# A hybrid RWKV-7 and DeltaNet block: a planner's landing times for loads, the order of its queue, and a read-back in pieces

## The chip, the cores and the metric

The kernel runs on one core of one Trainium2 chip. The metric is the time of one execution on the device in microseconds (us), the median of several. Engines are called PE (matrix products), DVE (vector), ACT (scalar, activations), POOL and SP; SP does nothing here but issue transfers.

## The reference

One layer of a diffusion backbone over 256 latent and 256 context tokens of width 2048, all in float32.

```python
mod = silu(c) @ w_ada + b_ada            # shifts, scales and gates of both halves
h  = modulate(rmsnorm(x, norm1_w), sh1, sc1)
hc = modulate(rmsnorm(ctx, norm1_w), csh1, csc1)
rw, cv, z, ab, gt = split(h @ w_in)      # and the same of hc
# branch 1: RWKV-7, 16 heads of 64, two directions, context scan first
s = s * w_t - (s @ kk_t) b_t^T + v_t k_t^T ;  y_t = s @ r_t
# branch 2: gated DeltaNet, 8 heads of 128, chunks of 64, two directions
sol = triangular_solve(I + lmat, [v*beta, k*beta*exp(g)])
v_new = u_i - w_i @ s ;  o = qd_i @ s + qk_i @ v_new ;  s = s * gl + kt_i^T @ v_new
m = sigmoid(g_a) * (o_a @ p_a) + sigmoid(g_b) * (o_b @ p_b)
x = x + gt1 * (m @ w_out)
x = x + gt2 * (silu(gate) * up) @ w_down # SwiGLU, hidden 5632
return rmsnorm(x, final_norm_w)
```

## The kernel before, in words

Every float32 product with a weight is done as three products of rounded halves: `whi` is the weight rounded by ACT, `wlo` the rest, subtracted by DVE, and the activation is split in the same way; PE multiplies whi with both halves and wlo with the first.

The program has four parts. First come the modulation of the first norm and the low-rank products (to about 125 us of the profile). Then a planned stretch (lines 1150 to 1830, 125 to 1340 us) does the input projection, both branches with their scans, and the first products of the merge. Then comes the rest of the merge with the output projection (to 1500 us), and last the feed-forward network (to the end). The last two are in a fixed order.

The planned stretch is written as some hundred generators, called pieces, each with a rank. The class `Weave` (line 218) runs them while the program is built: each yields its next operation, the planner keeps a clock for each engine and each piece, and at every step it takes the operation that could start first, the smaller rank first among equals. So a table of costs, `LAT` in line 31, sets the order in which PE, DVE, ACT and POOL run their instructions. On the chip each engine keeps to its row and waits by semaphores. A piece that yields a number waits for so long in planned time. The order of SP's queue is not the planner's own: it is made by the library's scheduler, which follows the order in which the issues are written and what they need.

`Loads` (line 168) stands for the queue. Called, it issues the transfer at once, and returns the planned time to its landing: from the later of now and the queue's free time, the bytes at 360 KB a us, and `LAT["dma"]`.

Pieces that the change touches:

- `fetch` and `cast` (lines 1156, 1164): weights come in quarters of 128x512 (256 KB) into a ring of buffers `raws`; ACT then makes whi (`his`) and DVE wlo (`los`).
- `gate_out` (1148): a product of the gates' columns is copied by ACT and stored to `gts_` in DRAM; `merge_gates` reads the gates back as `gts`.
- `merge_in` (1194): reads branch 1's output `oad` from DRAM into `PA` and splits it with `both` (a copy on ACT, a subtraction on DVE), so that the products with `pa` can start. Those with `pb`, branch 2, follow when its last head is done.
- `ada_early` (1754) and `ada_rest` with `row_tile` (1771): the rest of the modulation. Each transfer brings a row block of `ada_rest`, which DVE multiplies by an entry of `ck` and adds to the last one; there are 96 of 128x512 (tile `wraw`) and then 48 of 128x1024 (tile `aw`), all of rank 500. The early ones use two spare tiles, which afterwards go into the ring `raws` (it has three until then, and a third spare joins later).
- `invert` (635): the triangular inversions, with round trips through DRAM (`scr`, `tscr`).
- `head_inverse`, `head_scan`: a DeltaNet head's inversion, and its scan in four steps, in which PE (`s<-gvt,TF`, `s<-St,arena`), DVE (`Vn`), PE (`s<-Vn,kta`) and DVE (`St`) take turns, and `s<-Qe,St` with `s<-aw,Vn` give the output; `s<-arena,CR` then sums squares for the norm.

In names `out<-in,in` the products with a weight are `mm<-x,whi` and `mm<-x,wlo`; `ob` is branch 2's output. Line 164 is that of a helper which records every operation of a piece, line 175 that of `Loads`.

Of the kernel before, what the change touches and what calls it, by code (L numbers as in the profile page):

```python
# [27 lines left out]
NHELD, NB = 6, 10  # L28
GATES_A, GATES_B = ((36,0,0,0,0,0,0,0),(0,0,0,0,0,4,0,0))

LAT = dict(dma=3.1, v=1.0, s=1.0, hop=dict(e=0.215, v=0.135, s=0.15, g=0.1), slack=0.1, own=0.09, grp=32, crank=-1, cg=4, into=0.14, back=0.2, cross=0.14, stay=0.0, gpace=1.6)
LNEXP = "natural_log_exp_and_others"
SIGM = "sigmoid_and_others"
UNIT = 64 * 64 + 64
# [53 lines left out]
class Places:  # L88


    def __init__(self, pool, arena, *tags):
        self.pool, self.slots, at = pool, {}, 0
        for tag, n, bufs in tags:
            self.slots[tag] = itertools.cycle([arena[:, at + n * i:at + n * i + n] for i in range(bufs)])
            at += n * bufs
# [17 lines left out]
class Lane:  # L113


    def __init__(self, engine, fixed, each, own, hop):
        self.engine, self.fixed, self.each, self.own, self.hop, self.base = engine, fixed, each, own, hop + LAT["slack"], None

# [49 lines left out]
class Loads:  # L168
# [5 lines left out]
    def __call__(self, out, src, slow=1.0):  # L174
        self.queue.dma_start(out, src)
        cost = int(np.prod(out.shape)) * 4 / 360e3 * slow
        self.free = max(self.free, weave.now) + cost
        return self.free + LAT["dma"] - weave.now

# [38 lines left out]
class Weave:  # L218
# [52 lines left out]
    def turn(self, mode):  # L271
        return 0.0 if mode == self.mode else LAT["back"] if mode == "full" else LAT["into"] if self.mode == "full" else LAT["cross"]

    def run(self):
        while self.work:
# [4 lines left out]
            for w in self.work:  # L280
# [4 lines left out]
                elif isinstance(w.want, list):  # L285
                    lane = w.want[0].lane
                    start = max(self.free.get(lane, 0.0), w.at(lane))
                    if lane is self.tensor and self.mode != "full" and w.want[0].mode == "full":
                        start += LAT["stay"]
                    key = (start, w.rank)  # L290
# [16 lines left out]
            if lane is self.tensor:  # L307
                ops, rest = ops[:LAT['grp']], ops[LAT['grp']:]
                if self.mode == "full" and ops[0].mode == "full" and start > self.free.get(lane, 0.0) + 0.02:
# [19 lines left out]
def emit(ctx: ExitStack, tc, A, out, dbg=None):  # L329
    nc = tc.nc  # L330
    V, S, G, Q = nc.vector, nc.scalar, nc.gpsimd, nc.sync
    E = nc.tensor
    global weave
    weave = Weave()
    dq = Loads(Q)
    e, v, s, g = (Lane(x, fixed, each, LAT["own"], LAT["hop"][n]) for x, fixed, each, n in
                  ((E, 0.0, 0.0, "e"), (V, 0.07, 0.00104, "v"), (S, 0.06, 0.0009, "s"), (G, 0.06, 0.0022, "g")))
    e.own = 0.0
# [136 lines left out]
    with tc.tile_pool(name="p0", bufs=1) as p0, \  # L475
# [78 lines left out]
        def low_split(e):  # L554
            res = []
            for k in range(2):
                pool = p0 if e % 2 else wp
                pair = []
                for t in ("whi", "wlo"):
                    if t == "wlo" and e == k == 0:  # L560
                        V.memset(wp.tile([P, 32], F32, tag="wpad", name="wpad", bufs=1), 0.0)
                    pair.append(pool.tile([P, 8, P] if pool is wp else [P, NL], F32R, tag=f"{t}{k}" if pool is p0 else t, name=t,
                                          bufs=1 if pool is p0 else 2))
                hi, lo = pair
                if pool is wp:
                    hi, lo = (t.rearrange("p k m -> p (k m)")[:, :NL] for t in (hi, lo))
                S.copy(hi, lws[e][k])
                V.tensor_sub(lo, lws[e][k], hi.bitcast(F32))
                res.append((hi, lo))
            return res  # L570
# [13 lines left out]
        for part in range(NE + 1):  # L584
            if part < NE:
                ps = pst(pmm, "mm")
            for c in range(4):
# [4 lines left out]
                if c == 0 and part < NE:  # L592
                    w = low_split(part)
# [152 lines left out]
    oad = dpool.tile([8, P, T], F32, name="oad")  # L746
# [401 lines left out]
    def gate_out(pool, j, ps):  # L1148
        g = pool.tile([P, T], F32, tag="gt", name="gt")
        yield s.copy(g, ps[:, :T])  # L1150
        weave.release(mmb)
        Q.dma_start(gts_[j], g)
        if j == 39:
            weave.ready("gates")

    def fetch(parts, i):

        for q, part in enumerate(parts):
            raw = yield raws
            landed[i, q] = raw, weave.now + dq(raw[:, :part.shape[1]], part)  # L1160
            weave.ready("asked", i, q)
            yield 0.0
# [24 lines left out]
    OA, OB, PA, gts = [], [], [], []  # L1187

    def both(dst, src, i, n):

        yield s.copy(dst[0][:, i:i + n], src)
        yield v.tensor_sub(dst[1][:, i:i + n], src, dst[0][:, i:i + n].bitcast(F32))

    def merge_in():

        yield "out", NPAIR - 1
        for what in "KV":
            yield what + "gemm", NGH - 1
        oa = hx.tile([P, 2, 8, T], F32R, tag="ch", name="oa")
        OA.extend((oa[:, 0], oa[:, 1]))  # L1200
        PA.append(hx.tile([P, KT, T], F32, tag="cl", name="PA"))
        yield dq(PA[0][:, 0:8], oad.rearrange("k p t -> p k t"))
        for i in range(0, 8, 2):
            yield from both(OA, PA[0][:, i:i + 2], i, 2)
        weave.ready("merge")

# [48 lines left out]
    def products():  # L1255
# [53 lines left out]
        while todo or ahead:  # L1309
# [62 lines left out]
            if what == "g":  # L1372
                weave.add(150, gate_out(rs, p, ps))
            elif what == "p":
                weave.add(150, first_merge(p, ps, p == KT - 1))
            else:
                (hd if what in "KVQ" else pr)[p][what + "ps"] = ps
                weave.ready(what + "gemm", p)
# [360 lines left out]
    def ada_sum(b, nj, acc, arow):  # L1739

        m = 2 * nj
        ps = yield pab
        yield [e.matmul(ps[32 * j:32 * j + 32, 0:T], ones[:, 0:32], acc[:, T * j:T * j + T], start=True, stop=True)
               for j in range(nj)]
        weave.ready("block", b)
        r = slice(0, 32 * nj)
        yield v.tensor_copy(arow[r], ps[r, 0:T])
        yield [e.transpose(ps[:, T + P * q:T + P * q + 32 * nj], arow[r, P * q:P * q + P], ident[r, r]) for q in range(2)]
        for q in range(2):
            o = slice(32 + b + q, 32 + b + m, 2)  # L1750
            yield v.tensor_add(mod[:, o], ps[:, T + P * q:T + P * q + 32 * nj:32], p_("bada")[:, o])
        weave.release(pab)

    def ada_early():

        yield ("spare",)
        ws = [t.rearrange("p k m -> p (k m)") for t in spare[:2]]
        for b in range(NEARLY):
            for k in range(KT):
                w, last = ws[k % 2], ws[1 - k % 2]  # L1760
                yield dq(w, A["ada_rest"][b // 2, :, k, 512 * (b % 2):512 * (b % 2) + 512])
                if k:
                    yield v.scalar_tensor_tensor(w, w, ck[:, k, 0:1], last, ALU.mult, ALU.add)
                else:
                    yield s.activation(w, w, AF.Identity, scale=ck[:, 0, 0:1])
            yield from ada_sum(4 * b, 2, w, last[:, 0:T])
        raws.put(*spare[:2])
        yield "turned", NPAIR - 1
        raws.put(spare[2])

    def ada_rest():
        yield ("places",)
        yield "out", NPAIR - 1
        acc, kx = [gs.tile([P, 1024], F32, tag="KBc", name="aw") for _ in range(2)]
        ws = [gs.tile([P, 1024], F32, tag="KBm", name="aw") for _ in range(2)]
        for i in (0, 512):
            PTs.append(kx[:, i:i + 512].rearrange("p (d b c) -> p d b c", d=2, b=2))
        weave.ready("extra")
        arow = gs.tile([P, T], F32, tag="arow", name="arow")
        early = NEARLY // 2  # L1780

        def row_tile(i):
            b, k = divmod(i, KT)
            w = ws[i % len(ws)]
            yield dq(w, A["ada_rest"][b, :, k, :])
            if k == 0 and b > early:
                yield "block", 8 * (b - 1)
            if k:
                yield "added", i - 1
            for n in (0, 512):  # L1790
                a = acc[:, n:n + 512]
                if k:
                    yield v.scalar_tensor_tensor(a, w[:, n:n + 512], ck[:, k, 0:1], a, ALU.mult, ALU.add)
                else:
                    yield s.activation(a, w[:, n:n + 512], AF.Identity, scale=ck[:, 0, 0:1])
            weave.ready("added", i)

        for i in range(early * KT, 6 * KT):
            if i > early * KT + 1:
                yield "added", i - 2  # L1800
            weave.add(500, row_tile(i))
            if i % KT == KT - 1:
                yield "added", i
                weave.add(500, ada_sum(8 * (i // KT), 4, acc, arow))
# [28 lines left out]
    PA = PA[0]  # L1833
# [35 lines left out]
    with tc.manual_schedule(engines={mybir.EngineType.PE, mybir.EngineType.DVE, mybir.EngineType.Activation,  # L1869
# [18 lines left out]
        for j in range(KT):  # L1888
# [7 lines left out]
            k, a = divmod(j, 4)  # L1896
            raw = zap.tile([P, CG, P], F32, tag="wr", name="wr", bufs=2)
            k = slice(CG * k, CG * k + CG)
# [10 lines left out]
    with tc.tile_pool(name="fp", bufs=1, reuse_waits="tile") as fp:  # L1909
# [19 lines left out]
        for j in range(NH):  # L1929
# [6 lines left out]
            g = fp.tile([P, T], F32, tag="g", name="g", bufs=2)  # L1936
# [5 lines left out]
            if 2 <= j < 34:  # L1942

                for a in range(2):
                    c = (j - 2) // 2
                    i = 2 * (j % 2) + a
                    w = fp.tile([P, 512], F32, tag="aw", name="aw", bufs=3)
# [119 lines left out]
```

## Time and profile before

| what | value |
|---|---|
| median of 3 runs (lowest to highest) | 2208.12 us (2203.57 to 2210.75) |
| the profiled execution | 2211.11 us |
| its span | 2209.3 us |
| mean granted clock of PE | 0.986 |
| busy share of PE, DVE, ACT, POOL | 96%, 70%, 51%, 1% |

The span is the time between the first and the last instruction that the profile shows; busy shares are of the span. The granted clock is a share of the full one. A wait is shown at the instruction that waited, behind an arrow the engine and the tile that came last. `SPq` is SP's queue, PEld the loading of weights into PE.

### The profile page before, as it was taken

Reading aid. Unit: us, or ns where it says so; the run is one execution under the profiler, and the core shown is the slowest. Engines: PE = TensorE matmul, PEld = TensorE weight load, DVE = VectorE, ACT = ScalarE, POOL = GpSimd, SP = SyncE. Lnnn points to the kernel's source line nnn. Section 1 sums busy time; section 2 is a strip of 40 time slices with the busy share of each in tenths; the row PEclk is TensorE's granted clock in tenths of the full one; section 3 lists DMA queues with packets and bytes.
Section 4 is the critical chain, followed back from the end, with each engine's and each line's share of the span. In section 5 each row is a group of like instructions: output and inputs, shape, how many; then the busy total and the mean of one; then the engine's idle time right before and its main releaser. Section 6 shows DMA issues by size and latency. Waiting matters only on the chain. (4 is left out here: it accounts for less than half of the span.)

```text
span 2209.3 us, 59354 instructions
## 1 busy us (share of the span) xinstructions
PE 2124.0 (96%) x24654; PEld 1993.5 (90%) x24654; DVE 1554.4 (70%) x3318; ACT 1128.3 (51%) x2220; POOL 19.3 (1%) x55
## 2 busy tenths in 40 slices
PE   7999999999999999999999898999999999999998
PEld 4997698888899888898899898999999999999997
DVE  3466588888889877788888876765666665545554
ACT  3246554565556456655556564654444444444443
POOL 0000000000000000000000000000000000000000
PEclk9999999999999999999999999999999999999999
DMA  9966756645555564655556934846777776666665
GB/s 382 411 165 197 220 155 177 182 140 158 153 162 155 162 182 126 170 176 148 152 156 181 301 109 148 255 156 190 234 239 239 238 238 216 194 192 192 194 197 164
DMA packets 276286, 431.15 MB, mean 195 GB/s; under 512 B 119856, under 2 KB 136624, under 8 KB 271664
## 3 DMA queue, kind: packets, MB, share of 16 engines
q1 hardware_dynamic: 262192, 402.19, 59.3%
q10 hardware_dynamic: 13824, 25.17, 3.6%
q8 instruction: 193, 3.16, 0.6%
q14 instruction: 77, 0.63, 0.1%
HBM read 401.50 MB, written 25.77 MB: 193 GB/s over the span
## 5 line engine op out<-in xcount | busy, mean ns | idle before, releaser
L427 DVE TENSOR_TENSOR wlo<-wraw,whi 128x1024 fp32r<-128x1024 f32 (+1 forms) x264 | 315.0, 1193 | 297.3 <-ACT whi L426 297.1
L426 ACT CAST whi<-wraw 128x1024 fp32r<-128x1024 f32 (+1 forms) x264 | 270.6, 1025 | 391.0 <-PE mm L437 344.6
L164 PE MATMUL mm<-hxh,wlo 128*128 128x256 f32 x1376 | 401.8, 292 | 6.3 <-DVE wlo L164 5.8
L164 PE MATMUL mm<-hxh,whi 128*128 128x256 f32 x1376 | 398.2, 289 | 3.6 <-ACT whi L164 2.7
L164 PE MATMUL mm<-hxl,whi 128*128 128x256 f32 x1376 | 395.9, 288 | 0.2 <-issue 0.2
L438 PE MATMUL mm<-hfh,wlo 128*128 128x256 f32 x1344 | 372.8, 277 | 2.9 <-DVE wlo L427 2.9
L436 PE MATMUL mm<-hfh,whi 128*128 128x256 f32 x1344 | 371.2, 276 | 0.0
L437 PE MATMUL mm<-hfl,whi 128*128 128x256 f32 x1344 | 371.2, 276 | 0.0
L164 ACT CAST whi<-wraw 128x512 fp32r<-128x512 f32 (+1 forms) x398 | 243.1, 615 | 195.5 <-PE mm L164 80.0
L164 DVE TENSOR_TENSOR wlo<-wraw,whi 128x512 fp32r<-128x512 f32 (+1 forms) x398 | 269.7, 681 | 90.5 <-ACT whi L164 87.7
L164 PEld LDWEIGHTS mm<-hxh,wlo 128*128 128x128 f32 x1376 | 261.9, 190 | 18.4 <-DVE wlo L164 9.4
L164 PEld LDWEIGHTS mm<-hxh,whi 128*128 128x128 f32 x1376 | 261.7, 190 | 12.5 <-issue 4.5
L164 PEld LDWEIGHTS mm<-hxl,whi 128*128 128x128 f32 x1376 | 261.7, 190 | 5.9 <-issue 3.4
L438 PEld LDWEIGHTS mm<-hfh,wlo 128*128 128x128 f32 x1344 | 252.4, 188 | 5.1 <-DVE wlo L427 4.9
L437 PEld LDWEIGHTS mm<-hfl,whi 128*128 128x128 f32 x1344 | 252.5, 188 | 0.0
L436 PEld LDWEIGHTS mm<-hfh,whi 128*128 128x128 f32 x1344 | 252.5, 188 | 0.0
L164 PE MATMUL mm<-hch,wlo 128*128 128x256 f32 x496 | 143.5, 289 | 0.0
L164 PE MATMUL mm<-hch,whi 128*128 128x256 f32 x496 | 142.8, 288 | 0.0
L164 PE MATMUL mm<-hcl,whi 128*128 128x256 f32 x496 | 141.9, 286 | 0.1
L436 PE MATMUL mm<-za,whi 128*128 128x256 f32 x512 | 141.5, 276 | 0.0
L438 PE MATMUL mm<-za,wlo 128*128 128x256 f32 x512 | 141.3, 276 | 0.0
L437 PE MATMUL mm<-za,whi 128*128 128x256 f32 x512 | 141.3, 276 | 0.0
(399 smaller groups left out, 4585.9 us busy)
## 6 DMA issues: line engine op xcount, KB each, us to landing
wraw<-w SPq DMA_DIRECT2D x344, 256.0 KB, 3.3
wraw<-wgu SPq DMA_DIRECT2D x168, 512.0 KB, 4.8
aw<-ada_first SPq DMA_DIRECT2D x32, 1024.0 KB, 10.9
wraw<-wdn SPq DMA_DIRECT2D x64, 448.0 KB, 3.6
wraw<-ada_rest SPq DMA_DIRECT2D x96, 256.0 KB, 3.2
aw<-ada_rest SPq DMA_DIRECT2D x48, 512.0 KB, 4.2
wraw<-wout SPq DMA_DIRECT2D x64, 256.0 KB, 4.2
aw<-ada_gt ACTq DMA_DIRECT2D x64, 256.0 KB, 5.1
```

Source lines behind the costliest of these rows:

```text
L164: return Op(self, cost, lambda: getattr(self.engine, name)(out, *a, **k), mode, base)
L426: S.copy(hi[:, c, :M], raw[:, c, :M])
L427: V.tensor_sub(lo[:, c, :M], raw[:, c, :M], hi[:, c, :M].bitcast(F32))
L436: E.matmul(ps, hi, Xh[:, k, :n], start=first and i == 0, stop=False)
L437: E.matmul(ps, hi, Xl[:, k, :n], start=False, stop=False)
L438: E.matmul(ps, lo, Xh[:, k, :n], start=False, stop=last and i == len(wt) - 1)
```

## The change

All loads are counted as landing 0.5 us later (`dma` 3.1 to 3.6), and rows of the modulation 1.5 us later still (`late`). A `yield 0.0` ahead of an issue gives the turn back to the planner, so that the issues are written in the order of planned time; this is done for the weights, the gates' stores and the modulation rows. `gq` is the same queue as `dq`. The read-back of branch 1 is four transfers of two slices, each followed by its split, where it was one of eight slices.

```diff
-LAT = dict(dma=3.1, ..., gpace=1.6)
+LAT = dict(dma=3.6, ..., gpace=1.6, late=1.5)
...
-    dq = Loads(Q)
+    dq = gq = Loads(Q)
...
         yield s.copy(g, ps[:, :T])
         weave.release(mmb)
+        yield 0.0
         Q.dma_start(gts_[j], g)
...
             raw = yield raws
+            yield 0.0
             landed[i, q] = raw, weave.now + dq(raw[:, :part.shape[1]], part)
...
-        yield dq(PA[0][:, 0:8], oad.rearrange("k p t -> p k t"))
         for i in range(0, 8, 2):
+            yield dq(PA[0][:, i:i + 2], oad[i:i + 2].rearrange("k p t -> p k t"))
             yield from both(OA, PA[0][:, i:i + 2], i, 2)
...
                 w, last = ws[k % 2], ws[1 - k % 2]
-                yield dq(w, A["ada_rest"][b // 2, :, k, 512 * (b % 2):512 * (b % 2) + 512])
+                yield 0.0
+                yield LAT["late"] + gq(w, A["ada_rest"][b // 2, :, k, 512 * (b % 2):512 * (b % 2) + 512])
...
             w = ws[i % len(ws)]
-            yield dq(w, A["ada_rest"][b, :, k, :])
+            yield 0.0
+            yield LAT["late"] + gq(w, A["ada_rest"][b, :, k, :])
```

The instructions stay the same ones, but for three transfers more and one table load of ACT less. Their order in the planned stretch changes throughout. PE still has its 19501 products; of the full-size ones that precede the first RWKV inversion there are 656 where there were 692, and of those that precede the last DeltaNet head's inversion 6042 where there were 6016, of 6408. On SP the first early row of the modulation stands behind 47 weight loads, before behind 50, and the last one behind 315, before behind 275.

The end of the planned stretch on PE. Before, from the second to the fourth step of the last DeltaNet head's scan:

```order
L164 MATMUL s<-gvt,TF_12647 128x128
L164 MATMUL s<-St,arena 128x128
L164 MATMUL mm<-ob_18194,wlo 128x256
L164 MATMUL mm<-ob_18194,whi 128x256 x2
L164 MATMUL mm<-ob_18194,wlo 128x256
L164 MATMUL mm<-ob_18194,whi 128x256 x2
L164 MATMUL mm<-ob_18194,wlo 128x256
L164 MATMUL mm<-ob_18194,whi 128x256 x2
L164 MATMUL mm<-ob_18194,wlo 128x256
L164 MATMUL mm<-ob_18194,whi 128x256
L164 MATMUL s<-Vn,kta 128x128 x2
L164 MATMUL mm<-ob_18194,whi 128x256
```

There are 87 such products between this scan's steps. With the change the scan begins thus:

```order
L164 MATMUL mm<-ob_18099,wlo 128x256
L164 MATMUL s<-gvt,TF_12599 128x128 x2
L164 MATMUL s<-Vn,kta 128x128 x2
L164 MATMUL s<-gvt,TF_12599 128x128
L164 MATMUL s<-St,arena 128x128
L164 MATMUL s<-gvt,TF_12599 128x128
L164 MATMUL s<-St,arena 128x128
L164 MATMUL s<-Vn,kta 128x128 x2
```

It goes on so to `s<-arena,CR`, with nothing but the scan's own products. Those that stood between its steps stand earlier, beside the last head's inversion; 258 products with `ob` follow the scan in both.

SP, where branch 1 is read back (`tscr` and `iv` belong to an inversion). Before:

```order
L175 DMA aw<-ada_rest 128x1024
L175 DMA iv<-tscr_116 64x4x64
L175 DMA PA<-oad 128x8x256
L175 DMA iv<-tscr_116 64x4x64 x3
L175 DMA wraw<-w 128x512 x2
```

And with the change:

```order
L175 DMA aw<-ada_rest 128x1024
L175 DMA iv<-tscr_116 64x4x64 x3
L175 DMA aw<-ada_rest 128x1024
L175 DMA iv<-tscr_116 64x4x64
L175 DMA wraw<-w 128x512
L175 DMA PA<-oad 128x2x256 x4
L175 DMA wraw<-w 128x512
```

The four pieces stand together, behind the whole round trip of that inversion and one weight load.

SP, where the gates go out and come back. Before:

```order
L175 DMA gts<-gts__1615 128x2x256 x2
L1152 DMA gts__1615<-arena 128x256
L175 DMA aw<-ada_rest 128x1024
L175 DMA gts<-gts__1615 128x2x256 x3
L175 DMA wraw<-pa 128x512
```

And with the change:

```order
L175 DMA wraw<-pa 128x512 x6
L175 DMA gts<-gts__1615 128x2x256
L1153 DMA gts__1615<-arena 128x256
L175 DMA gts<-gts__1615 128x2x256 x4
L175 DMA wraw<-pa 128x512
L175 DMA aw<-ada_rest 128x1024
L175 DMA gts<-gts__1615 128x2x256 x6
```

The last store of a gate, which waits for ACT's copy, stands behind one load of gates where it was behind two, and the row of the modulation that was right behind it stands after the next four loads of gates.

More of the change, by code (lines that the diff above doesn't have):

```diff
@@ L29 @@
 GATES_A, GATES_B = ((36,0,0,0,0,0,0,0),(0,0,0,0,0,4,0,0))
-LAT = dict(dma=3.1, v=1.0, s=1.0, hop=dict(e=0.215, v=0.135, s=0.15, g=0.1), slack=0.1, own=0.09, grp=32, crank=-1, cg=4, into=0.14, back=0.2, cross=0.14, stay=0.0, gpace=1.6)
+LAT = dict(dma=3.6, v=1.0, s=1.0, hop=dict(e=0.215, v=0.135, s=0.15, g=0.1), slack=0.1, own=0.09, grp=32, crank=-1, cg=4, into=0.14, back=0.2, cross=0.14, stay=0.0, gpace=1.6, late=1.5)
 LNEXP = "natural_log_exp_and_others"
```

## The prediction

> **What bounds the kernel now.** I read the totals first, then the busy time by stage, then what each engine waits for inside the planned stretch, and last the timeline around the longest of those waits.
>
> ```profile
> span 2209.3 us, 59354 instructions
> PE 2124.0 (96%) x24654; PEld 1993.5 (90%) x24654; DVE 1554.4 (70%) x3318; ACT 1128.3 (51%) x2220; POOL 19.3 (1%) x55
> ```
>
> The span lies in a run of 2211.1 us, so 1.8 us lie around it. The median of the runs, 2208.1, is 3.0 lower; I sum differences and take them from the median. PE is busy 96% of the time, so only PE's idle time and the clock it is granted can move much. Next, busy time by stage (us, then PE, PEld, DVE, ACT, POOL, the granted clock, the DMA share, GB/s):
>
> ```profile
> 125.00:260.00 135.00, 125.42 (x909) 100.98 (x909) 80.57 (x176) 84.12 (x157) 2.42 (x7) 0.97 0.65 199
> 260.00:950.00 690.00, 670.60 (x10330) 611.27 (x10328) 588.02 (x1395) 385.12 (x963) 16.42 (x43) 0.99 0.56 160
> 950.00:1200.00 250.00, 242.37 (x2976) 227.97 (x2975) 220.41 (x603) 146.96 (x320) 0.00 (x0) 0.99 0.55 159
> 1200.00:1340.00 140.00, 128.41 (x1553) 120.37 (x1553) 106.02 (x285) 83.23 (x184) 0.00 (x0) 0.95 0.64 198
> 1340.00:1500.00 160.00, 153.79 (x1270) 150.02 (x1269) 110.90 (x204) 86.39 (x154) 0.00 (x0) 0.98 0.58 180
> 1500.00:2209.00 709.00, 695.53 (x6098) 692.87 (x6098) 395.58 (x511) 307.08 (x380) 0.00 (x0) 0.99 0.68 212
> ```
>
> The planner writes the order from 125 to 1340 us; what follows is in a fixed order and the change leaves it as it is. In that stretch PE is busy 1166.8 of 1215 us: 48.2 us idle, plus what the clock loses (0.95 and 0.97 at its two ends). No better plan can bring more than that. What PE, DVE and ACT wait for there (us in total, times, longest; PE and DVE from 260 to 1340, the first ACT row to 950, the second after it):
>
> ```profile
> PE pi L164 <- DVE extra L164: 4.7, 2, 2.5
> PE mm L164 <- DVE wlo L164: 3.4, 8, 1.0
> PE s L164 <- ACT R L164: 3.3, 2, 1.9
> PE s L164 <- DVE Vn L164: 2.8, 2, 2.5
> PE mm L164 <- ACT whi L164: 2.3, 6, 0.7
> ...
> DVE wraw L164 <- DMA wraw<-ada_rest: 21.4, 15, 3.4
> DVE aw L164 <- DMA aw<-ada_rest: 6.9, 3, 4.6
> ...
> ACT whi L164 <- DMA wraw<-w: 56.7, 33, 5.0
> ...
> ACT oa L164 <- DMA PA<-oad: 3.6, 1, 3.6
> ```
>
> DVE stands 28.3 us in 18 waits for modulation rows, ACT 56.7 us in 33 for weights. Both engines have slack (70% and 51% busy), so what counts is how much of this comes out on PE.
>
> **T1, modulation rows counted as longer.** A row of 256 KB was planned to land 0.73 + 3.1 = 3.83 us after its turn; now 0.73 + 3.6 + 1.5 = 5.83. A row of 512 KB goes from 4.56 to 6.56. Each row's addition is thus put 2.0 us later on DVE, which then does other work first. The loads themselves are not slow:
>
> ```profile
> wraw<-w SPq DMA_DIRECT2D x344, 256.0 KB, 3.3
> wraw<-ada_rest SPq DMA_DIRECT2D x96, 256.0 KB, 3.2
> aw<-ada_rest SPq DMA_DIRECT2D x48, 512.0 KB, 4.2
> PA<-oad SPq DMA_DIRECT2D x1, 1024.0 KB, 7.0
> ...
> L175 SPq DMA_DIRECT2D wraw<-ada_rest x96: 327/328/2904, 249.6 to 949.8; - x96
> ```
>
> 3.2 and 4.2 us from issue to landing are less than the plan gave before, so the waits come from rows issued late on SP; an allowance covers that just as well. Where DVE's wait comes out on PE, the timeline shows in pairs, the row's addition and then PE's gap (in brackets the idle time before, and what ended it):
>
> ```profile
> 930.46 0.75 DVE L164 SCALAR_TENSOR_TENSOR wraw<-wraw,ck 128x512 f32<-128x512 f32 x1 [2.98 <-DMA wraw<-ada_rest]
> 933.21 0.44 PE L164 MATMUL pi<-extra,LT 32*32 32x16 f32 x32 [2.16 <-DVE extra L164]
> ...
> 1083.09 0.75 DVE L164 SCALAR_TENSOR_TENSOR aw<-aw,ck 128x512 f32<-128x512 f32 x1 [1.88 <-DMA aw<-ada_rest]
> 1085.92 0.70 PE L164 MATMUL s<-arena,CR 128*128 128x256 f32 x2 [0.99 <-ACT arena L164]
> ...
> 1243.97 0.75 DVE L164 SCALAR_TENSOR_TENSOR aw<-aw,ck 128x512 f32<-128x512 f32 x1 [4.56 <-DMA aw<-ada_rest]
> 1247.72 0.49 PE L164 MATMUL s<-aw,Vn 128*128 128x128 f32 x2 [2.47 <-DVE Vn L164]
> ```
>
> An allowance 2.0 us longer takes 2.0 + 0.99 + 2.0 = 5.0 us of these three gaps. The clock drops around them:
>
> ```profile
> 925.00:940.00 15.00, 12.84 (x212) 12.20 (x211) 11.79 (x29) 6.67 (x18) 0.00 (x0) 0.89 0.76 208
> 1075.00:1097.00 22.00, 19.05 (x318) 17.33 (x317) 20.00 (x51) 10.20 (x27) 0.00 (x0) 0.95 0.45 112
> 1240.00:1267.00 27.00, 21.47 (x269) 19.95 (x271) 21.06 (x50) 12.56 (x27) 0.00 (x0) 0.91 0.89 284
> ```
>
> 0.11 x 15 + 0.05 x 22 + 0.09 x 27 = 5.2 us lost; other pauses lie there too, so I take half, 2.5. DVE's backlog behind the other 15 waits I put at 1. T1 = -8.5, between 0 (the row is issued later by as much) and -11 (all of the clock as well).
>
> **T2, weights counted 0.5 us longer.** ACT's 33 waits have a mean of 1.7 us; 0.5 covers 30% of it. PE's share of them is 3.4 (wlo) + 2.3 (whi) + 3.3 (R, which stands behind the casts on ACT) = 9.0, of which 30% is 2.7; the clock adds about 0.8. T2 = -3.5, between 0 and -9 (all of it).
>
> **T3, the end of the planned stretch.** In the new order the last GDN head's inversion has full-size products beside it, and its scan, the last chain before the branch-2 products, has none: 87 of them stood between its steps. So each of its steps shows its own latency on PE. Before, its last step alone stood nearly bare:
>
> ```profile
> 1331.74 0.38 PE L164 MATMUL s<-gvt,TF 128*128 128x128 f32 x2
> 1332.83 0.61 DVE L164 TENSOR_SCALAR Vn<-s,btok 128x128 f32<-128x128 f32 x2 [2.58 <-PE s L164]
> 1333.70 0.38 PE L164 MATMUL s<-Qe,St 128*128 128x128 f32 x2
> 1338.91 1.04 PE L164 MATMUL mm<-ob,whi 128*128 128x256 f32 x2 [2.43 <-ACT ob L164]
> ...
> 1330.00:1345.00 15.00, 11.54 (x75) 10.78 (x74) 7.46 (x16) 4.62 (x10) 0.00 (x0) 0.77 0.43 149
> 1900.00:1950.00 50.00, 50.00 (x444) 50.00 (x443) 25.31 (x28) 21.97 (x28) 0.00 (x0) 1.00 0.60 194
> ```
>
> From DVE's start at 1332.83 to the next products of the scan at 1333.70 is 0.9 us; with four steps of two halves, less the first and the last, six such pauses are new: +5.4. The granted clock of 0.77 there says that short pauses in a row cost clock; one half-speed stretch of 3.4 us more, as 0.23 x 15 = 3.4 us is lost around the old end, costs half of it, +1.7. T3 = +7. Low end +5.4, no clock. High end: the scan takes as long as the 87 products that covered it, 87 x 0.113 us (50 us over 444) = 9.8, and 3.4 for clock: +13.
>
> The Trainium skill, page "TensorE: Matmul & The Clock Gate", section "HAM oscillation", has it that the clock falls where PE idles for more than about 3.4 us. By that rule pauses of 0.9 us cost no clock, T3 would be its low end and the whole sum -5.6. The trace does not agree: the clock fell to 0.77 in a stretch whose longest idle time is 2.43 us, so the measurement decides and the 1.7 stays.
>
> **T4, buffers returned later.** The early modulation rows use two spare weight buffers, and until they finish the weight ring has three. In the queue's order the last early row stands behind 315 weight loads, before behind 275: 40 loads later. The rows began behind 50 loads, so from 249.6 to 949.8 us 225 weight loads went past, 3.1 us each, so the ring is short for 124 us more. In that regime (690 us) PE's 9.0 us of T2 arise; 124/690 of it is 1.6. T4 = +2, between 0 and +4 (twice that, as the products last in line need their weights fastest).
>
> **T5, the read-back in four pieces of 256 KB.** ACT waits 3.6 us once for the 1 MB read that takes 7.0; pieces land earlier, like the 3.3 of a weight load. PE shows no gap behind that wait, because products of other pieces are queued: 0, between 0 and -1. Three more issues on SP of 0.33 us are hidden in its waits. A table load fewer lies in ACT's slack: 0.
>
> **T6, gate stores and loads in planned order.** SP waits for ACT before it may store gates, and what stands behind on SP waits too:
>
> ```profile
> SPq L1152 <- ACT arena L164: 14.7, 14, 3.4
> ```
>
> 14.7 us in 14 waits, mean 1.05; the planned order puts each store after its copy. Most of what is behind has a buffer's slack. T6 = -1, between 0 and -3.
>
> Sum: -8.5 - 3.5 + 7 + 2 + 0 - 1 = -4, or 2204 on the median (2207 on the profiled run's basis).
>
> **Rivals.**
> R1, slower. The bare scan decides: it costs its high end, +13, while rows and weights give half, -4.25 and -1.75, T4 +2, T6 0: +9, 2217. For it: 87 products vanish from between its steps, and the clock is already at 0.77 there. Against: the work is not lost, the products stand beside the inversion instead. It turns slower than a measurement can miss once T3 exceeds 10.6.
> R2, no change: the allowance doesn't cover anything. The pause put in front of each issue moves it to its planned time, so that issue and landing shift together with the addition that waits for them, T1 = T2 = 0; and the last inversion, with products beside it, gives back T3 out of the idle 11.6 us of 1200 to 1340. T4 +2 and T6 -1 stay: 2209. For it: landings were already shorter than planned, so the lateness is SP's. Against: the pairs above, where DVE was placed too early.
> R3, the full gain: T1 -11, T2 -9, T3 +5.4, T4 0, T6 -3: -17.6, 2191. For it: 48.2 us of idle PE and all three pairs come from loads. Against: a new plan makes new gaps of its own.
>
> **How the numbers follow.** From no change a measurement of this kernel tells about 0.3%, 6.6 us: faster below 2201.5, slower above 2214.7. The forecast has 0.45, with 2198 to 2212 as its own range: as its centre is inside the bound and T1 alone spans 11 us, 0.19 of it falls faster, 0.24 the same, 0.02 slower. R3 0.17, faster. R2 0.18, the same. R1 0.20, slower. Together 0.36, 0.42, 0.22. The range goes from 2192, nearly R3's time, to R1's 2217; beyond each end lies about 0.1.
>
> **What would show it.** T1: DVE's waits for the two kinds of modulation rows, 28.3 us, fall below 12, and no PE gap over 1.5 us follows one. T2: ACT's wait for weights falls from 56.7 to about 40, PE's for whi and wlo from 5.7 to 4. T3: some 10 us ahead of the branch-2 products in which PE stands idle half of the time between pairs of scan products, clock under 0.8. T4: the last early row issued after about 1000 us instead of 949.8. T5: ACT's wait for the read-back under 1.5 us. T6: SP's wait for ACT ahead of gate stores under 5. The prediction is wrong if the planned stretch, now ending near 1340, ends before 1325 or after 1350.

## The result and the profile after

| what | before | changed |
|---|---|---|
| median, on the same chip | 2208.12 us | 2214.09 us (9 runs, 2211.11 to 2221.5) |
| ratio to before (95% interval) | | 1.0046 (1.0024 to 1.0068) |
| profiled execution, its span | 2211.1, 2209.3 us | 2216.8, 2215.0 us |
| mean granted clock of PE | 0.986 | 0.981 |

The change makes the kernel slower by 0.46%, about 10 us, where -4 us was forecast. The ratio is taken over the fast runs of both kernels; the two medians alone differ by 6.0 us. The same stretches as before:

```profile
125.00:260.00 135.00, 124.84 (x920) 99.50 (x922) 79.99 (x174) 83.46 (x154) 3.62 (x7) 0.99 0.65 197
260.00:950.00 690.00, 672.69 (x10321) 612.51 (x10316) 581.69 (x1385) 383.19 (x961) 17.63 (x43) 0.98 0.54 153
950.00:1200.00 250.00, 245.07 (x3081) 231.91 (x3080) 222.60 (x605) 148.25 (x330) 0.00 (x0) 0.99 0.54 159
1200.00:1340.00 140.00, 127.50 (x1423) 118.39 (x1421) 110.25 (x284) 78.37 (x168) 0.00 (x0) 0.90 0.75 235
1340.00:1500.00 160.00, 150.82 (x1236) 147.26 (x1237) 110.98 (x209) 83.72 (x153) 0.00 (x0) 0.97 0.58 180
1500.00:2209.00 709.00, 702.13 (x6167) 700.06 (x6165) 396.33 (x514) 311.67 (x386) 0.00 (x0) 1.00 0.68 210
```

Up to 1200 us PE is idle a little less than before (17.3 us instead of 19.4 in the second row, 4.9 instead of 7.6 in the third). The loss is in the fourth and fifth: fewer products done (x1423, before x1553), and a clock of 0.90 instead of 0.95.

One cut makes it plain. The last product of the input projection starts at 1222.0 us, before at 1222.4. The last branch-2 product starts at 1383.1, before at 1374.6. So nothing was won in 1222 us, and 8.9 us were lost in the 160 after them: that part, called the tail below, is 161.1 us long instead of 152.2.

What DVE waits for rows of the modulation, and when the rows are issued (the two kinds, first and last start; then who waited, in us and times):

```profile
L175 SPq DMA_DIRECT2D wraw<-ada_rest x96: 327/328/1987, 244.3 to 1109.3; - x96
L175 SPq DMA_DIRECT2D aw<-ada_rest x48: 327/328/1400, 878.0 to 1313.9; - x48
...
  DVE wraw L164: 0.4, 1
  DVE aw L164: 0.4, 1
```

The waits are gone, 0.8 us where 28.3 were. But each row depends on the one before it, so 2 us more for each has stretched the whole series: the early rows end at 1109 instead of 950, the late ones at 1314 instead of 1253. The late rows now lie beside the last DeltaNet head. There the last solve, 30 small steps on DVE (`arena<-arena`, 64 partitions), stands between them. Its first and last steps before, and then in the changed kernel:

```profile
1274.56 0.16 DVE L164 TENSOR_TENSOR arena<-arena 64x15 f32<-64x15 f32 x1
...
1287.67 0.16 DVE L164 TENSOR_TENSOR arena<-arena 64x15 f32<-64x15 f32 x1
```

```profile
1268.68 0.16 DVE L164 TENSOR_TENSOR arena<-arena 64x15 f32<-64x15 f32 x1
1268.77 0.74 DVE L164 SCALAR_TENSOR_TENSOR aw<-aw,ck 128x512 f32<-128x512 f32 x1
...
1291.82 0.74 DVE L164 SCALAR_TENSOR_TENSOR aw<-aw,ck 128x512 f32<-128x512 f32 x1
...
1293.69 0.36 DVE L164 TENSOR_TENSOR arena<-arena 64x15 f32<-64x15 f32 x2
```

The solve starts 6 us earlier and ends 6 later: 25.4 us instead of 13.3. The groups of DVE between 1262 and 1294 us, two of before and then the same two of the changed kernel, say what stands between its steps:

```profile
L164 DVE TENSOR_TENSOR arena<-arena 64x15 f32<-64x15 f32 (+7 forms) x30 | 5.9, 197 | 0.8
L164 DVE SCALAR_TENSOR_TENSOR aw<-aw,ck 128x512 f32<-128x512 f32 x2 | 1.4, 708 | 0.0
```

```profile
L164 DVE SCALAR_TENSOR_TENSOR aw<-aw,ck 128x512 f32<-128x512 f32 x12 | 8.8, 738 | 0.0
L164 DVE TENSOR_TENSOR arena<-arena 64x15 f32<-64x15 f32 (+7 forms) x30 | 5.8, 193 | 0.3
```

The solve's own work is about the same, 5.8 us. Two of the 12 additions of rows (at 1264.32 and 1266.73 us) stand ahead of the solve; the other ten, 7.4 us, stand between its steps, where none stood before. So do twelve steps of another head's scan (`Vn` and `St`), 4.0 us. PE meanwhile uses up the products that could have covered the last scan, and that scan stands bare:

```profile
1330.31 0.60 PE L164 MATMUL s<-gvt,TF 128*128 128x128 f32 x4
1332.42 0.46 PE L164 MATMUL s<-Vn,kta 128*128 128x128 f32 x2 [1.50 <-DVE Vn L164]
1334.06 0.80 PE L164 MATMUL s<-St,arena 128*128 128x128 f32 x2
1336.16 1.22 PE L164 MATMUL s<-Vn,kta 128*128 128x128 f32 x4 [0.44 <-DVE Vn L164]
1346.82 0.70 PE L164 MATMUL s<-arena,CR 128*128 128x256 f32 x2 [1.10 <-ACT arena L164]
1349.95 0.38 PE L164 MATMUL mm<-ob,whi 128*128 128x256 f32 x1 [2.43 <-ACT ob L164]
```

And the stretch from 1299 to 1347 us as a row of busy times, before and then in the changed kernel:

```profile
1299.00:1347.00 48.00, 42.83 (x530) 40.24 (x520) 33.70 (x85) 20.96 (x50) 0.00 (x0) 0.93 0.31 98
1299.00:1347.00 48.00, 40.57 (x468) 35.34 (x468) 33.41 (x80) 15.82 (x40) 0.00 (x0) 0.79 0.46 137
```

The pauses are short, 1.50 us at most up to 1347 us, but at 1334 us a pair of products takes 0.80 us where a pair took 0.38 before: the clock, 0.79 over 48 us, is a good part of the loss. Only half of that belongs to the bare scan. In the trace's clock records the clock is either full or half; it is half from 1333.8 to 1344.0 us, inside the scan, and just as long from 1303.0 to 1313.3 us, ahead of it, where PE waits four times for `ob` from DVE (2.8 us, the longest 1.0).

### The profile page after: what moved, and what is told of

It is laid out like the page before. It is cut to its first block, busy times and chain, and to the rows that moved or that the text cites. A ratio compares the mean times of both kernels' runs of the same rounds, so it can differ in the third digit from the quotient of the medians.

```text
span 2215.0 us, 59336 instructions
## 1 busy us (share of the span) xinstructions
PE 2130.4 (96%) x24654; PEld 1999.3 (90%) x24654; DVE 1558.3 (70%) x3318; ACT 1125.5 (51%) x2219; POOL 21.7 (1%) x55
## 4 chain that ended last, share of the span: by engine, by line
PE 78%; DMA 8%; DVE 7%; ACT 4%; issue 2%; SPq 1%; ACTq 0%; DVEq 0%
PE mm L164 26%; PE mm L438 12%; PE mm L436 11%; PE mm L437 11%; PE s L164 7%; PE pa L164 5%; PE pi L164 2%; DMA wraw<-w 2%; DVE arena L164 2%; DVE wlo L164 2%; DMA wraw<-wgu 2%; PE mm L529 1%; ACT whi L164 1%; PE s L579 1%; DMA tscr<-arena 1%
```

## The experiments

Theory A says that the late rows, made later by their own allowance, slow the last head on DVE; theory B that the longer planned round trips of the inversions (3.6 us) put that head late; theory C that the bare scan costs little. D came with experiment 4.

All were timed against the kernel before on the same chip; the ratio with its 95% interval is given, and the median. The front, below, is the stretch up to the start of the last projection product, the tail the time from there to the start of the last branch-2 product, both from the one profiled execution. Two of these, before and 7, share their order up to 1180 us and differ by 4.5 us in the front, so a smaller difference there says nothing. The profiled execution need not be a middle one: that of before took 3.0 us more than its median, those of 4, 6, 11 and 12 took 5.7 to 7.7 us less than theirs, so their fronts and tails hold only part of their loss. The ranges in the expectations start from 2208.1 us; on the chips of the experiments the kernel before had medians of 2203.8 to 2205.7 us.

| kernel | ratio (interval) | DVE's waits for rows | front | tail |
|---|---|---|---|---|
| before | 1 | 28.3 us | 1222.4 | 152.2 |
| changed | 1.0046 (1.0024 to 1.0068) | 0.8 | 1222.0 | 161.1 |
| 1 rows held back | 1.0020 (1.0008 to 1.0033) | 1.2 | 1221.8 | 151.6 |
| 2 one read | 1.0033 (1.0019 to 1.0046) | 2.4 | 1220.4 | 158.3 |
| 3 allowance alone | 1.0060 (1.0038 to 1.0082) | 5.7 | 1223.8 | 159.1 |
| 4 turns alone | 1.0092 (1.0070 to 1.0113) | 16.6 | 1240.2 | 148.9 |
| 5 plan at 3.15 | 1.0089 (1.0065 to 1.0113) | 23.9 | 1241.3 | 146.0 |
| 6 plan at 3.05 | 1.0056 (1.0032 to 1.0079) | 30.9 | 1225.6 | 152.5 |
| 7 pieces alone | 0.9994 (0.9980 to 1.0009) | 29.7 | 1217.9 | 150.3 |
| 8 no allowance | 1.0004 (0.9991 to 1.0016) | 11.1 | 1217.9 | 150.7 |
| 9 rows by POOL | 1.0023 (1.0005 to 1.0040) | 24.7 | 1228.7 | 148.1 |
| 10 changed, rows by POOL | 1.0056 (1.0038 to 1.0074) | 1.4 | 1220.9 | 160.2 |
| 11 early rows' allowance | 1.0059 (1.0039 to 1.0079) | 2.3 | 1226.8 | 155.0 |
| 12 allowance, short trips | 1.0092 (1.0073 to 1.0111) | 0.0 | 1231.4 | 155.2 |

**1, the late rows held back from the last solve.** The changed kernel with

```diff
             b, k = divmod(i, KT)
+            if i >= 84:
+                yield "solved", NGH - 1
             w = ws[i % len(ws)]
```

> The changed kernel, in which the last 12 of the modulation's 48 late rows may start only when the last DeltaNet head's solve (30 small steps on DVE) is done; the planned order up to that solve is the same. Theory A (the later rows stand on DVE inside the last solve, which took 25.3 us instead of 13.1, so the products that should cover the last scan are used up before it): the solve takes 12 to 16 us, the scan has 111 products between its steps, the 13 us lost after 1300 us come back nearly whole: 2201 to 2206. Theory B (the longer planned round trips of the inversions put the last head late): they stay as they are, 2212 to 2216, and the scan is covered but the head is as late as before. Theory C (the bare scan cost little, the loss is elsewhere): 2212 or more with a covered scan.

2209.42 us. The solve's steps lie between 1267.5 and about 1278.3 us:

```profile
1267.53 0.16 DVE L164 TENSOR_TENSOR arena<-arena 64x15 f32<-64x15 f32 x1
...
1277.73 0.58 DVE L164 TENSOR_TENSOR arena<-arena 64x28 f32<-64x28 f32 x3
```

The solve takes 10.8 us, less than A's 12 to 16 (the other head's scan steps now stand behind it too); the tail is 9.5 us shorter than in the changed kernel and as long as before, with the front as it was. Over the runs 0.26% came back, some 6 us of the 10 (by the two ratios, whose intervals still overlap). Theory A holds for the tail. Theory B does not: the planned round trips were the same 3.6. But it is still slower than before, beyond A's range.

**2, one read.** The changed kernel with `yield dq(PA[0][:, 0:8], ...)` ahead of the loop again.

> The changed kernel with the read-back of branch 1 in one piece again. The planned order is the same up to the sixth DeltaNet solve; behind it 4 row additions stand in the last solve (10 in the changed kernel), and 87 products between the steps of the last scan (none). Theory A: 2203 to 2207, the tail as in the kernel before, and 24 row additions behind the solve cost at most 2 us. Theory B (planned round trips): the same 3.6 is planned, 2212 to 2216. If the read-back in pieces has a worth of its own, ACT's wait for it, 3.6 us before, comes back here without a gap on PE.

2213.43 us: A missed. The last scan is covered by 87 products, and the tail is 158.3 us all the same. PE's timeline shows where,

```profile
1334.49 0.63 PE L164 MATMUL pa<-aw,CR 128*32 128x256 f32 x4 [1.53 <-DVE aw L164]
1335.75 0.78 PE L164 MATMUL pa<-aw,CR 128*32 128x256 f32 x4 [0.64 <-DVE aw L164]
1337.06 0.69 PE L164 MATMUL pa<-C,arow 128*128 128x128 f32 x2 [0.52 <-DVE arow L164]
1337.54 0.63 PE L164 MATMUL s<-Qe,St 128*128 128x128 f32 x2
```

and DVE's shows what they wait for:

```profile
1333.68 0.75 DVE L164 SCALAR_TENSOR_TENSOR aw<-aw,ck 128x512 f32<-128x512 f32 x1 [2.04 <-DMA aw<-ada_rest]
```

The last row lands late inside the last scan; the products that sum up the rows wait for it on PE (1.53, 0.64 and 0.52 us), and the scan's last products stand behind them. So late rows beside the last head reach PE without a bare scan too. These three waits come to 2.7 us, though, and the tail is 6.1 us longer than before. Part of the rest is clock (0.68 from 1330 to 1347 us, 0.80 before); that all of it comes from the rows is not shown.

**3, the allowance alone; 4, the turns alone.** The kernel before with `late=1.5` and `yield LAT["late"] + dq(...)` at both kinds of rows; and the kernel before with the four `yield 0.0` only.

> The kernel before with the rows' allowance of 1.5 us alone (loads planned at 3.1, no turn given back, one read). 9 row additions stand in the last solve and 8 products in the last scan. Theory A: DVE's waits for rows fall from 28.3 to under 8 us, the last scan is nearly bare, and the time is 2210 to 2217. Theory B: the round trips are planned as before, so the last head is as early as before, and with the waits gone 2198 to 2204.

> The kernel before with the turns given back ahead of loads and gate stores alone (3.1, no allowance, one read). No row addition stands in the last solve and 92 products in the last scan. Theory A: the tail as in the kernel before, waits for rows still 20 to 30 us: 2204 to 2212. A theory in which the order of the queue alone brings or costs the difference: 2214 or more, or 2200 or less.

2218.30 and 2227.71 us. The first is slower than A expected, with its tail long (159.1) and its front no shorter, though 22.6 us of waits for rows are gone. The second has a clean tail, 148.9, and comes out 20 us slower, all of it in the front. A doesn't explain that, and its 20 to 30 us of waits for rows were 16.6. The other theory written there, that the order alone brings or costs the difference, fits, and led to a theory D: any other order of the planned stretch loses by itself.

**5 and 6, other orders by a hair of one cost.** `dma=3.15` and `dma=3.05` in the kernel before. The first is a tenth of the change's own step in `dma`, the second as much the other way.

> The kernel before with one number changed: loads planned at 3.15 us instead of 3.10. It has no step of the change, yet the planned order is another one throughout; no row addition stands in the last solve and 102 products in the last scan. Theory A (each loss has its place: the rows in the last solve, waits moved elsewhere): within 3 us of the kernel before. Theory D (the order before is a good draw among many, and any other order loses by itself some 5 to 20 us, in clock and in new gaps, which hides what the change brings): 2210 to 2225.

> The same the other way, 3.05 us instead of 3.10: another order again, no row addition in the last solve, 90 products in the last scan. Theory A: within 3 us of the kernel before. Theory D: 2210 to 2225, and not the same as the run with 3.15.

2223.49 and 2217.73 us, 20 and 12 us slower for 0.05 us in a planning cost, both with clean tails. D holds and A is out for these. For the first, the stretch from 260 to 950 us shows it, by busy times (before 670.60 us of PE) and by PE's longest sums of waits:

```profile
260.00:950.00 690.00, 660.23 (x10126) 599.89 (x10126) 578.55 (x1365) 375.45 (x942) 17.65 (x43) 0.99 0.57 159
```

```profile
PE pi L164 <- issue: 5.5, 6, 2.7
PE pa L164 <- ACT arena L164: 4.6, 2, 3.5
PE pa L164 <- ACT gate L164: 3.3, 2, 2.8
PE mm L164 <- issue: 3.1, 2, 2.1
```

PE is idle 29.8 us instead of 19.4, in single waits of up to 3.5 us on things that no term of the prediction touches.

**7, the pieces alone.** The kernel before with the read-back in four pieces.

> The kernel before with the read-back in four pieces alone. The order is the same up to about 1180 us, and 87 products stand in the last scan in both. Theory A and D alike: the end of the planned stretch within 2 us, ACT's wait for the read-back under 2 us instead of 3.6, the time within 3 us of the kernel before. If the pieces by themselves cost (three more issues on SP between inversions' round trips): 3 us or more slower.

2202.93 us, no change. ACT's wait for the read falls from 3.6 to 0.7:

```profile
ACT oa L164 <- DMA PA<-oad: 0.7, 1, 0.7
```

**8, the changed kernel without the allowance** (`late=0.0`).

> The changed kernel with the rows' allowance at 0 (3.6 for all loads, turns, four pieces). No row addition stands in the last solve and 102 products in the last scan. Theory A: the last scan as in the kernel before, DVE's waits for rows come back to 10 us or more, no more than 1 us of gap each on PE: 2204 to 2210. Theory D: somewhere in 2210 to 2225, whatever the rows do.

2205.52 us, the same as before. A's range holds, D's doesn't: not every other order loses. The allowance is the whole difference between this and the changed kernel, 0.42% or some 9 us. In the two profiled executions the changed kernel's tail is 10.4 us longer and its front 4.1 us longer; that is more, as one took 2.8 us more than its median and the other 4.0 less.

**9 and 10, the rows issued by POOL.** `dq(..., queue=G)` for the 144 rows, with planned costs untouched; PE, DVE and ACT keep their order, of the kernel before and of the changed one.

> The kernel before, in which POOL issues the 144 modulation rows and SP nothing of them; PE, DVE and ACT run their instructions in the very same order as before. So it shows what rows that land sooner are worth without a new order, the first term of the prediction by itself. The term as predicted, -8.5 (0 to -11): DVE's 28.3 us of waits for rows fall under 8, the three PE gaps of 2.16, 0.99 and 2.47 us go, 2193 to 2200. If the waits are nearly all beside the path: DVE's waits fall as well, and the time is within 3 us of the kernel before. POOL has some 50 memsets that may stand behind an issue that waits; if they do, new waits of DVE for POOL appear and it is slower.

> The changed kernel with the same edit, PE, DVE and ACT in the order of the changed kernel (up to the feed-forward network). DVE waits 0.8 us for rows there, so nothing is to be had from them; SP is rid of 103 us of waits for row buffers that weight loads stand behind. If those are what makes weights late: ACT's waits for weights fall from 60 us to under 40 and the time by 3 us or more, 2203 to 2210. If not: within 3 us of the changed kernel, 2210 to 2216, with its last scan bare as it was.

2210.57 and 2217.30 us. The first is 0.23% slower with three engines in the same order; what costs that was not followed up. DVE still waits 24.7 us for rows, so it doesn't measure what rows that land sooner are worth; that stays open. Why they stay late is shown by POOL's waits before its issues:

```profile
POOL wraw L175 <- DVE wraw L164: 298.2, 52, 14.8
POOL aw L175 <- DVE aw L164: 166.1, 23, 22.2
```

These two, 464 us in 75 waits, are more than half of what POOL waits ahead of the rows' issues. There a row is issued when DVE has freed its buffer, and another queue doesn't make it earlier. In the second ACT's waits for weights are shorter, 47.1 us of 260 to 1340 where the changed kernel has 52.4 up to 950 and 7.6 behind it, and the time is no better (under 40 was written for the waits):

```profile
ACT whi L164 <- DMA wraw<-w: 47.1, 31, 4.1
```

**11, the allowance for the early rows alone; 12, loads planned at 3.1 and rows allowed 2.0.** The changed kernel with `late` left out in `row_tile`; and with `dma=3.1, late=2.0`.

> The changed kernel with the allowance of 1.5 us for the 96 early rows alone, none for the 48 late ones. The early rows' waits should be gone as in the changed kernel, the late rows end before the last solve is over (6 additions in it, none behind it), 73 products stand in the last scan. Theory A (the loss is the late rows beside the last head): 2203 to 2208, against 2205.5 with no allowance at all. Theory D (an order costs what its gaps and its clock come to, which no term of the change sets): no forecast but the spread of the runs so far, 2203 to 2225; before 1222 us its idle time and its clock decide.

> The changed kernel with loads planned at 3.1 and rows allowed 2.0: the rows are planned to land when they are in the changed kernel, weights and the inversions' round trips as in the kernel before. 2 row additions stand in the last solve, 28 behind it, 95 products in the last scan. Theory A: covered scan, 2203 to 2209, a few us for the additions behind the solve as with the rows held back (4 us). Theory B (planned round trips of 3.6 make the loss): 2203 or less. Theory D: 2203 to 2225.

2218.62 and 2225.61 us. A missed both. In 12 no row is waited for at all, and it is among the slowest; B is out by it as well. The tails, 155, lie between the clean ones and that of the changed kernel; the rest is in the fronts, 4 to 9 us longer than before.

Over all kernels the tail goes with the row additions that stand between the steps of the last solve, counted in the traces. In before, 1, 4, 5, 6, 7, 8 and 9 there is one or none, and the tail is 146.0 to 152.5 us; in the changed kernel, 2, 3, 10, 11 and 12 there are two to ten, and it is 155.0 to 161.1 us. Additions behind the solve don't do it: 1 has 24 of them. Nor does a covered scan prevent it: 87, 73 and 95 products stand in the last scans of 2, 11 and 12. This bears A out for the tail, and says nothing on the fronts.

No kernel here is faster than before. Eight runs have an order of their own (the changed kernel, 3, 4, 5, 6, 8, 11, 12): seven are slower by 0.46 to 0.92%, one is the same. The four with an allowance have a mean of 0.64%, the four without one 0.60%. So the change's 0.46% is no more than another order costs; experiment 8 ties it to the allowance, and experiment 1 a part of it to the late rows.

## Why the prediction was wrong

The forecast was 4 us faster, and the kernel is slower. The median, 2214.1, lies in the range; the time by the ratio, 2208.1 x 1.0046 = 2218, lies just above its end, near the rival R1 (2217, with a chance of 0.20). R1 comes near by luck: it gave rows and weights half their worth and the bare scan 13 us, while the first two brought nothing and the whole tail lost 8.9. T3's total is about what was written; the sum turned over because T1 and T2, -12 together, came to nothing.

- **T1, -8.5, gave nothing.** Its sign in the profile came as written: DVE's waits fell below 12 us, to 0.8. But the front is as long as before, and kernels with 0.0 to 30.9 us of these waits show no relation between them and the time. Experiment 3 is the rows' allowance by itself: the waits fall to 5.7 us, and the time is 0.60% longer. The step that failed is the one from three gaps of a profile to the sum: it took the gaps away and put nothing in their place. PE's wait for `extra` did go, from 4.7 to 0.9 us, and from 125 us to the end of the front PE is idle 33.1 us where it was 37.3. But the clock is at half speed for 41.0 us there, before 30.7, which costs up to 5.1 us; experiment 7, which shares the order of before up to 1180 us, differs from it by as much (20.5 us). A new order has gaps of its own: in the changed kernel PE waits up to 2.4 us for a late weight and 3.9 for an inversion's round trip. Its waits of 260 to 1340 us:

```profile
PE pi L164 <- DMA extra<-tscr: 4.2, 2, 3.9
PE mm L164 <- ACT whi L164: 3.4, 3, 2.4
```

  And the granted clock (third from the end of a row) is 0.66 and 0.62 in two stretches where it was 1.00 and 0.91 (two rows of before, then the same two of the changed kernel):

```profile
495.00:515.00 20.00, 19.48 (x448) 18.46 (x447) 17.89 (x42) 7.68 (x16) 0.85 (x2) 1.00 0.71 200
727.00:745.00 18.00, 16.94 (x465) 15.39 (x465) 16.73 (x33) 6.18 (x13) 0.45 (x2) 0.91 0.61 188
495.00:515.00 20.00, 16.54 (x437) 14.75 (x439) 12.51 (x25) 4.80 (x11) 0.00 (x0) 0.66 0.34 102
727.00:745.00 18.00, 15.57 (x363) 13.99 (x364) 13.09 (x24) 5.20 (x12) 0.32 (x2) 0.62 0.43 138
```

  "A new plan makes new gaps of its own" stood in the text, but only against R3, with no price. Experiments 5 and 6 give it: 20 and 12 us, more than any term of the sum.
- **T3, +7, came nearly as sized, in part by luck:** the tail is 8.9 us longer. PE is idle 3.9 us more in it (+5.4 was written) and busy 5.0 us more: its clock is at half speed for 34.1 us, before 17.1, so for five stretches of 3.41 us more where one was written, and three of the five lie ahead of the bare scan. The sign written for the scan came by half: from 1330 to 1347 us the clock is 0.70, but PE is idle 4.2 of 17 us, a quarter and not half. T3's cause was not seen. It was taken for an accident of the order, and is an effect of T1: T4 counted what the longer series of rows does to the weight ring, and nothing counted what it does to DVE in the last head. Experiment 1 shows that cause, and prices it at 9.5 us of tail in one profile, 0.26% over the runs.
- **T2, -3.5, gave nothing that shows.** ACT's waits for weights are 60.0 us (before 57.0), PE's for `whi` and `wlo` 4.8 (before 5.7). SP waits longer for the buffers that the weights are to go in, 298.8 us where it was 251.3. That fits R2, by which the issue shifts with the landing; `dma=3.6` was not tried by itself. SP's waits, the first line before, the others in the changed kernel:

```profile
SPq L175 <- DVE wlo L164: 251.3, 172, 6.6
...
SPq L175 <- DVE wlo L164: 298.8, 179, 10.5
...
SPq L1153 <- ACT arena L164: 29.3, 24, 5.3
```

- **T4's sign came** (last early row at 1109 us, written was after 1000); its price can't be told from the rest.
- **T5, 0, was right:** experiment 7.
- **T6, -1, was wrong in its sign:** SP's wait ahead of gate stores was to fall under 5 us and rose from 14.7 to 29.3. What that costs was not tried by itself.
- **The clock.** The Trainium skill, page "TensorE: Matmul & The Clock Gate", section "HAM oscillation", ties the fall of the clock to idle gaps beyond about 3.4 us; here it fell to 0.79 in a stretch whose longest wait of PE is 1.50 us. The choice against the rule was right, and the 1.7 us taken for it too little for the tail as a whole.

What stays open is why one order loses 12 to 20 us and another none: idle time and clock tell where (from 125 us to the end of the front PE is idle 46 to 51 us in 4, 5 and 12, before 37.3; in 3 the clock is at half speed for 44.4 us, before 30.7), but no rule was found that tells it ahead.

## What to carry to other kernels

When a planner's costs are changed, the first thing to price is another order as such: change a cost by a hair with no purpose, two or three times, and see the spread before reading anything into the change. An allowance for a serial chain of transfers is paid at every link, so ask where the chain now ends and what it stands beside there. A wait that an engine off the path loses is worth only what the path shows, and that is read at a fixed point of the work (the last product of a stage), not from the waits.

## What was not expected of the hardware

PE's clock fell without a long pause: in the bare scan it was at half speed from 1333.8 to 1344.0 us behind waits of 1.50 us and less, and a pair of 128x128 products took 0.80 us instead of 0.38. Apart from the last one of each run, the half-speed stretches in the profiles of before and of the changed kernel last 3.41 us or a multiple of it, up to 13.65. The issue of a 256 KB row took 536 ns of POOL's time where SP shows 328.
